# A two-layer diffusion trunk on one core: soft pauses for the modulation's steps, an earlier place for layer 1's, and layer 0's first query projection beside the values

## The chip, the core and the metric

The kernel runs on one core of one Trainium2 chip. The metric is the device time of one execution in microseconds (us), lower is better. Before the change the median of 3 runs is 2235.13 us (2232.56 to 2236.04).

## What is computed

The reference is one inference step of a trunk of two layers, each with its own weights, on 128 prompt tokens and 512 latent tokens (640 columns here), with D = 1024 channels in fp32:

```python
def trunk_layer(x, cond, p, ctx):
    mod = jax.nn.silu(cond) @ p['w_mod'] + p['b_mod']
    sh1, sc1, g1, sh2, sc2, g2 = [m[:, None, :] for m in jnp.split(mod, 6, axis=-1)]
    h = rms_norm(x, p['g_attn']) * (1 + sc1) + sh1
    a, new_ctx = mixer_sublayer(h, p, ctx)
    x = x + g1 * a
    h = rms_norm(x, p['g_ffn']) * (1 + sc2) + sh2
    x = x + g2 * conv_ffn(h, p)
    return x, new_ctx
```

`mod`, the **modulation**, is six vectors of 1024 numbers for each of two conditions; its matrix is 1024 by 6144, 24 MB for each layer. The mixer projects h to the inputs of three branches (a: neighbourhood attention, b: grouped-query attention, c: gated linear attention, which takes `qc`, `kc`, `vc`, `rc`), gates the three results, adds them and projects the sum with `w_out`. `conv_ffn` is an up projection to 2 x 2816 channels, a convolution of width 3, a gate, and a down projection.

## The kernel before

**Layout.** Activations lie with channels on the 128 partitions and the 640 tokens in the free dimension, as 8 blocks. A large product is made of three fp32r matmuls (high x high, high x low, low x high parts), 320 columns wide; weights are loaded as 512 KB tiles by the SP queue, split into a high part on ACT and a low part on DVE or POOL (`Weights.fetch`, `make`, L564), a few tiles ahead of use.

**Who sets the order.** The program is written as streams, Python generators which yield what they wait for: a tile, a free buffer, or an `Event` (L195) with a time. `Order` keeps a modelled clock for each engine, and `Order.one` (L355) picks the next stream: the first in order of priority (0 before 1 before 2 before 3) whose waits are over at the modelled TensorE time, or else the one whose waits end first. The engines then run the instructions in the order so chosen; the model's times are not the chip's. The main stream has priority 2. `Order.later` (L324) gives an event so many ns after the present TensorE time, a **pause**.

**Buffers.** `U` hands out 49 work buffers of 128 x 648 fp32 (4 more at times). A stream that finds none free waits for one to be given back. PSUM has the banks `MM` (2, with 4 more in some stages), `TB` (2) and `S2`.

**The modulation.** `Mod.first` (L748) makes layer 0's first two vectors in four quarters, at the program's start. `Mod.rest` (L782) makes others: `ring` is two pairs of work buffers, each pair holding one block k of one vector (two loads of 256 KB), and a fifth buffer `ms` collects the sums, five `U` buffers held to the end. One step takes two blocks k: it waits for all four loads and for the pause, issues 4 matmuls for each block (128 partitions, 32 columns of weights, 256 columns, one on each quarter of the array), then asks for the next two blocks. After the eighth block `finish` (L825) transposes the vector (two transposes, `modt`) into `modT`. For layer 0, `rest` makes four vectors with a pause of 4000 ns at priority 1. For layer 1 it makes all six, 48 blocks, through `next_mod` (L2285): it begins when `calm` is set, just before the first `bb` product of layer 0's branch b (L1829), with priority 3 and no pause; when the FFN reaches the second of its five parts of the down projection, `rush` (L2154) makes `hurry` (L2292) raise it to priority 1 with a pause of 2000 ns.

```python
            for i in range(0, len(todo), 2):
                v, k0 = todo[i]
                yield ring[0] + ring[1] + [cT, od.later(self.pause)]
```

**The stages.** In each layer: the norm gives h in blocks (`modulate`); `mixer` (L1702) first makes the values and gate inputs, `vz`, block by block of h as the blocks come; then `qc`, `kc`, `rc` twice, and the rest of the branches; branch b ends with `bb`; then the output projection `wo`; then the FFN: two raw blocks (`up`), a norm and `factors` (L931), the other blocks as `pair_x`, `pair_w`, `pair_y` with `pair_act` (L2060), and `dn`, the down projection, whose last part leads into the next layer. In layer 1 the first `qc` and `kc` are made ahead of the norm (`evac_raw`); in layer 0 they come behind `vz`.

Of the kernel before, what the change touches and what calls it, by code (L numbers as in the profile page):

```python
# [18 lines left out]
P = 128  # L19
D = 1024  # L20
KC = 8
# [4 lines left out]
HT = 320  # L26
# [106 lines left out]

def weight_plan(plan, l):

    full = slice(0, D)
    cols = lambda c0, n=P: slice(c0, c0 + n)
    at = lambda nm, r, c: (nm, l, r, c)
    one = lambda c0: plan.plain([at("w_in", full, cols(c0))], KC)
    first = [c0 + p * P for p in range(2) for c0 in (1536, 1792, 2304)]  # L140
    early = NRAW if l else 0
    for c0 in first[:early]:
        one(c0)
    for kk in range(4):
        r = cols(kk * 256, 256)
        plan.plain([at("w_in", r, cols(2048, 256)), at("w_in", r, cols(2560, 32))], 2)
    for c0 in first[early:]:
        one(c0)
    for i in range(KC):
        one(4640 + i * P)  # L150
    for p in range(2):
        for c0 in (0, 256, 512):
            one(c0 + p * P)
    for i in range(0, KC, 4):
        plan.plain([at("w_branch_c", slice(0, 256), cols(i * P, 4 * P))], 2)
    for c0 in (1280, 1408, 768, 896, 1024, 1152):
        one(c0)
    for c0, nm, nk in ((2592, "a", 2), (3616, "b", 4)):
        for kind, i in branch_steps(nm):
            if kind == "g":  # L160
                one(c0 + MERGE[i] * P)
            elif i % (KC // nk) == 0:
                plan.plain([at("w_branch_" + nm, slice(0, nk * P), cols(MERGE[j] * P)) for j in range(i, i + KC // nk)],
                           nk)
    for o in range(KC):
        plan.plain([at("w_out", full, cols(o * P))], KC)
    up = lambda c: [at("ffn_w_up", full, cols(c * P))]
    for step in ffn_steps():
        if step[0] == "raw":
            plan.plain(up(step[1] + step[2] * NFF), KC)  # L170
        elif step[0] == "dn":
            b0, nb = FFN_PARTS[step[1]]
            plan.plain([at("ffn_w_down", cols(b0 * P, nb * P), cols(step[2] * P))], nb)
        else:
            i = step[1]
            plan.pair(step[0], (l, "up", i), (up(i), up(i + NFF)), KC)
# [17 lines left out]

class Event:  # L195
    time = INF


class Slot:
# [65 lines left out]
class Order:  # L265
# [55 lines left out]
        e.time = t  # L321
        return e

    def later(self, ns):  # L324

        return self.moment(self.at["PE"] + ns)

    def start(self, gen, prio):
        self.seq += 1
        self.streams.append([prio, self.seq, gen, ()])  # L330
        self.streams.sort(key=lambda s: s[:2])

    def lift(self, gen, prio):
        for s in self.streams:
            if s[2] is gen:
                s[0] = prio
        self.streams.sort(key=lambda s: s[:2])

    def step(self, s):
# [13 lines left out]
            self.one()  # L353

    def one(self):  # L355
        now, best, at = self.at["PE"], None, INF
        for s in self.streams:
            r = max((self.ready(x) for x in s[3]), default=0.0)
            if r <= now:
                best = s  # L360
                break
            if r < at:
                best, at = s, r
        if best is None:
            raise RuntimeError("streams wait for each other: " + str(
                [(s[2].__name__, [getattr(x[0], "tag", x) if isinstance(x, tuple) else type(x).__name__ for x in s[3]])
# [12 lines left out]
def kernel(ctx: ExitStack, tc: tile.TileContext, I, O, depth=2):  # L379
# [359 lines left out]

    class Mod:  # L740
        def __init__(self, l, pc=None, ready=None):
            self.l, self.pc, self.ready, self.pause = l, pc, ready, 0.0 if l else 4000.0
            self.T = prm.tile([P, 48, 2], F32, tag="modT", bufs=2, name=f"modT{l}")
            self.gsc = prm.tile([P, 2, KC, 2], F32, tag="gsc", bufs=2, name=f"gsc{l}")
            self.have = [Event() for _ in range(24)]
# [2 lines left out]
        def first(self, q):  # L748
# [28 lines left out]
            yield [acc]  # L777
            act(ms[:, :P], acc[:, :P])
            del acc
            yield from self.finish(ms, pieces, P, 256)  # L780

        def rest(self, vectors, after, whole):  # L782

# [11 lines left out]

            fetch(0)
            fetch(1)
            for i in range(0, len(todo), 2):  # L800
                v, k0 = todo[i]
                yield ring[0] + ring[1] + [cT, od.later(self.pause)]
                if k0 == 0 or not whole:
                    acc = yield from TB("mod")
                    psum_names.add(acc.ap.tensor.name)
                a, b = (0, KC - 1) if whole else (k0, k0 + 1)
                for j in range(2):
                    for g in range(4):
                        mm(acc[32 * g:32 * g + 32, :256], cT[:, k0 + j, :], ring[j][g // 2][:, g % 2 * 256:g % 2 * 256 + 256],
                           k0 + j == a, k0 + j == b, tile_position=(0, 32 * g))  # L810
                if not whole or k0 == KC - 2:
                    yield [acc]
                    if whole or k0 == 0:
                        act(ms[:, :256], acc[:, :256])
                    else:
                        tt(ms[:, :256], acc[:, :256], ms[:, :256], ADD)
                    del acc
                for j in range(2):
                    if i + 2 + j < len(todo):
                        yield [od.until(ring[j][1].ap)]  # L820
                        fetch(i + 2 + j)
                if k0 == KC - 2:
                    yield from self.finish(ms, (v * D,), 256, D)

        def finish(self, ms, pieces, n, wide):  # L825
            t = yield from TB("modt")
            yield [ms, self.ready]
            nx = n // P
            for x in range(nx):
# [872 lines left out]
    def mixer(l, h, pc, wg, raws, full, finish, calm):  # L1702
# [12 lines left out]
        merged = tiles8("xm", "mg", NT, F32)  # L1715
        od.start(side.serve(ub, NUX), 0)

        acc = []
        for t in range(5):
            acc.append((yield from MM("vz")))  # L1720
        for kk in range(4):
            w = yield from ws.next()
            for k in range(2):
                kx = kk * 2 + k
                yield [h.done[kx]]
                for t in range(5):
# [2 lines left out]
                    mm(o, h.hi[kx][:, c], w[0][:, k], kx == 0, False)  # L1729
                    mm(o, h.hi[kx][:, c], w[1][:, k], False, False)  # L1730
                    mm(o, h.lo[kx][:, c], w[0][:, k], False, kx == KC - 1)
        vc = [(yield from U("vc0")), (yield from U("vc1"))]
        zT = yield from U("zTs")
        zdone = Event()
# [5 lines left out]
        for p in range(2):  # L1740
# [1 line left out]
                q, k = ready  # L1742
                ready.clear()
            else:
                q = yield from U("qc")
                w = yield from ws.next()
                yield from proj_halves(w, X, KC, evac_to(q, 0.125), "qc")
                k = yield from U("kc")
                w = yield from ws.next()
                yield from proj_halves(w, X, KC, evac_to(k), "kc")  # L1750
# [367 lines left out]
        z = yield from pair_act(i, c, pc, ah)  # L2118
        yield from keep_split(i, z, ah, al, have)

    def ffn(l, x, raws, h, pc, mod, ss, nxt, nraws, rush):
        ah, al = {}, {}
        have = [Event() for _ in range(NFF)]
        pairs = {}
# [11 lines left out]
        for step in ffn_steps():  # L2136
# [13 lines left out]
            elif kind == "dn":  # L2150
                part, o = i, step[2]
                b0, nb = FFN_PARTS[part]
                if part == 1:
                    rush.time = 0.0  # L2154
                ks = range(b0, b0 + nb)
                a = [ah.get(k) for k in ks], [al.get(k) for k in ks]
                while None in a[0]:
# [58 lines left out]
    def program():  # L2216
# [20 lines left out]
        for l in range(depth):  # L2237
# [3 lines left out]
            if l == 0:  # L2241
                yield [h.done[0]]
            if l == 0:
                od.start(mod.rest((2, 3, 4, 5), mod.have[3], False), 1)
            nxt = None
            if l + 1 < depth:
                nxt = Mod(l + 1)
            lazy = next_mod(nxt, calm)
            od.start(lazy, 3)
            od.start(spill(x, h.done[KC - 1]), 1)  # L2250
            full, x = [Event() for _ in range(KC)], [None] * KC

# [21 lines left out]
                ss, nraws = SumSq(), Raw()  # L2274
            else:
                ss = nraws = None
            rush = Event()
            if nxt is not None:
                od.start(hurry(nxt, lazy, rush), 1)
            yield from ffn(l, x, raws, h, pc, mod, ss, nxt, nraws, rush)  # L2280
            raws = nraws
            if nxt is not None:
                mod, pc, wg = nxt, nxt.pc, nxt.wg
# [1 line left out]
    def next_mod(nxt, after):  # L2285
        yield [after]
        if nxt is not None:
            nxt.pc, nxt.wg, nxt.ready, work = load_params(nxt.l)
            od.start(work, 1)
            yield from nxt.rest(range(6), after, True)  # L2290

    def hurry(mod, lazy, when):  # L2292
        yield [when]
        mod.pause = 2000.0
        od.lift(lazy, 1)

    def spill(x, ready):
        yield [ready]
# [65 lines left out]
```

## Time and profile before

| | |
|---|---|
| median of 3 runs | 2235.13 us (2232.56 to 2236.04) |
| the profiled execution's own time | 2225.76 us |
| its span | 2224.0 us |
| TensorE, share of the span busy | 95% |
| VectorE, ScalarE, GpSimd | 70%, 50%, 10% |
| mean granted TensorE clock | 0.989 of full speed |
| DMA | 209.33 MB, mean 94 GB/s |

In the rows PE is TensorE's matmuls, PEld its weight loads, DVE VectorE, ACT ScalarE, POOL GpSimd, SP the engine that issues most DMAs. A row of the timeline has start and duration in us, engine, line, operation, tile written and tiles read, how many instructions are merged, and in brackets the engine's idle time before and who ended it. An fp32 matmul leaves two records, so a block of the modulation leaves 8 (`x8`), and the two transposes of a vector (`modt`) 2.

### The profile page before, as it was taken

To read this page: it belongs to the slowest core of one execution; us is meant where nothing else is said; L and a number is where in the kernel's file an instruction comes from. 1 tells how busy PE (TensorE), PEld (TensorE's weight loads), DVE (VectorE), ACT (ScalarE), POOL (GpSimd) and SP (SyncE) were. 2 spreads that over 40 slices of the span, in tenths; PEclk is the share of its full clock that TensorE was granted. 3 is DMA by queue.
4 is the path that set the end of the run, shared out by engine and by line. 5 is a ranking of instruction groups with operands and counts; after the bars stand their busy time and mean duration, and the time that the engine had idled before them with its cause. 6 is when DMAs were issued, how large, how long until landed. Compare 5 with 4: busy or idle time off the path is not lost. (4 is left out here: it accounts for less than half of the span.)

```text
span 2224.0 us, 40076 instructions
## 1 busy us (share of the span) xinstructions
PE 2113.6 (95%) x16208; PEld 1978.6 (89%) x16208; DVE 1561.9 (70%) x2827; ACT 1122.2 (50%) x2063; POOL 212.6 (10%) x283
## 2 busy tenths in 40 slices
PE   6999999999998968999999999999999989999999
PEld 4878988899997826999998989888999988999999
DVE  5376679673579804978777876787745798687785
ACT  4355755553356402544556667455532575445452
POOL 0201010000120001010010110100001200100101
PEclk9999999999999989999999999999999999999999
DMA  9752221112324373222223112211114212232212
GB/s 307 258 182 76 69 64 50 39 48 69 112 81 152 112 246 107 90 78 94 77 65 133 62 54 70 72 51 39 39 57 133 76 39 68 76 98 71 95 65 91
DMA packets 85874, 209.33 MB, mean 94 GB/s; under 512 B 9590, under 2 KB 22518, under 8 KB 85688
## 3 DMA queue, kind: packets, MB, share of 16 engines
q1 hardware_dynamic: 84472, 204.66, 28.7%
q8 instruction: 128, 2.10, 0.4%
q0 software_dynamic: 1216, 2.10, 0.3%
q14 instruction: 58, 0.48, 0.1%
HBM read 197.81 MB, written 10.98 MB: 94 GB/s over the span
## 5 line engine op out<-in xcount | busy, mean ns | idle before, releaser
L454 ACT ACTIVATE w_h<-w_st 128x1024 fp32r<-128x1024 f32 (+4 forms) x292 | 273.7, 940 | 220.0 <-PE dn L445 57.5
L470 DVE TENSOR_TENSOR w_h<-w_st,w_h 128x1024 fp32r<-128x1024 f32 (+4 forms) x253 | 276.7, 1095 | 140.1 <-ACT w_h L454 133.9
L445 PE MATMUL dn<-a_hi,w_h 128*128 128x320 f32 x1408 | 321.4, 310 | 1.1 <-ACT a_hi L454 1.1
L445 PE MATMUL pair_x<-f,w_h 128*128 128x320 f32 x1440 | 230.1, 311 | 11.1 <-ACT f L454 5.7
L445 PEld LDWEIGHTS dn<-a_hi,w_h 128*128 128x128 f32 x1408 | 239.4, 189 | 1.3 <-ACT a_hi L454 1.3
L445 PEld LDWEIGHTS pair_x<-f,w_h 128*128 128x128 f32 x1440 | 216.1, 189 | 14.1 <-ACT f L454 5.9
L445 PE MATMUL dn<-a_lo,w_h 128*128 128x320 f32 x704 | 218.4, 310 | 2.6 <-DVE a_lo L470 2.6
L445 PEld LDWEIGHTS dn<-a_lo,w_h 128*128 128x128 f32 x704 | 133.2, 189 | 2.8 <-DVE a_lo L470 2.8
L482 DVE SCALAR_TENSOR_TENSOR x<-dn,modT,x 128x128 f32<-128x128 f32 (+2 forms) x240 | 97.2, 434 | 54.4 <-PE dn L445 54.1
L445 PE MATMUL gc<-h_hi,w_h 128*128 128x320 f32 x512 | 131.8, 324 | 2.1 <-ACT mg L454 2.1
L445 PE MATMUL ga<-h_hi,w_h 128*128 128x320 f32 x512 | 125.9, 316 | 0.0
L473 POOL TENSOR_TENSOR w_h<-w_st,w_h 128x1024 fp32r<-128x1024 f32 (+3 forms) x39 | 78.3, 2008 | 470.8 <-ACT w_h L454 308.4
L445 PE MATMUL gb<-h_hi,w_h 128*128 128x320 f32 x512 | 119.0, 312 | 0.0
L445 PE MATMUL wo<-m_hi,w_h 128*128 128x320 f32 x768 | 113.0, 309 | 0.0
L445 PEld LDWEIGHTS wo<-m_hi,w_h 128*128 128x128 f32 x768 | 112.8, 188 | 0.0
L445 PE MATMUL mod<-mod,cT 128*32 128x256 f32 x640 | 76.0, 412 | 31.1 <-DMA mod<-in_w_mod_dram 29.8
L445 PEld LDWEIGHTS gc<-h_hi,w_h 128*128 128x128 f32 x512 | 89.0, 189 | 9.5 <-ACT mg L454 3.1
L445 PEld LDWEIGHTS mod<-mod,cT 128*32 128x32 f32 x640 | 21.1, 111 | 78.2 <-DMA mod<-in_w_mod_dram 65.2
L445 PEld LDWEIGHTS ga<-h_hi,w_h 128*128 128x128 f32 x512 | 88.1, 188 | 2.4 <-issue 2.4
L454 ACT ACT_TABLE_LOAD x64 | 82.1, 1283 | 16.0 <-PE hss L445 11.1
L445 PEld LDWEIGHTS gb<-h_hi,w_h 128*128 128x128 f32 x512 | 86.8, 188 | 1.6 <-issue 1.4
L445 PE MATMUL pair_x<-f_hi,w_h 128*128 128x320 f32 x320 | 79.3, 316 | 5.7 <-ACT up_a L454 5.7
(414 smaller groups left out, 5350.4 us busy)
## 6 DMA issues: line engine op xcount, KB each, us to landing
w_st<-in_wt_dram SPq DMA_DIRECT2D x204, 512.0 KB, 3.4
mod<-in_w_mod_dram SPq DMA_DIRECT2D x160, 256.0 KB, 3.8
w_st<-in_wt_dram SPq DMA_DIRECT2D x48, 320.0 KB, 3.0
mod_w<-in_w_mod_dram SPq DMA_DIRECT2D x32, 256.0 KB, 6.4
xd<-x SPq DMA_DIRECT2D x16, 320.0 KB, 6.0
x<-xd SPq DMA_DIRECT2D x16, 320.0 KB, 3.2
w_st<-in_wt_dram SPq DMA_DIRECT2D x16, 256.0 KB
w_st<-in_wt_dram SPq DMA_DIRECT2D x16, 192.0 KB, 2.5
```

The lines of the kernel that those rows point to most:

```text
L445: nc.tensor.matmul(out, lhsT, rhs, start=start, stop=stop, **kw)
L454: r = nc.scalar.activation(out=out, in_=in_, func=f, **kw)
L470: nc.vector.tensor_tensor(out, a, b, op=op)
L473: nc.gpsimd.tensor_tensor(out, a, b, op=op)
L482: nc.vector.scalar_tensor_tensor(out=out, in0=a, scalar=s, in1=b, op0=op0, op1=op1)
```

## The change

Pauses of the modulation become `Soft` events. `Order.one` looks first for a stream that is ready with all its waits; when there is none, it looks again and leaves soft waits out, so a stream that waits for its pause alone is taken before TensorE would stand idle. Layer 1's modulation gets priority 1 and a pause of 3000 ns from `calm` on, and takes one block k at a time (`n = 1`), while the other half of the ring is being loaded; `rush`, `hurry` and `lift` go. Layer 0's keeps two blocks and 4000 ns, now soft. In layer 0 the first `qc` weight tile moves to the front of the weight plan, ahead of those of `vz`; its 6 matmuls for each block of h are issued behind the 15 of `vz`, into the two `TB` banks, and its separate pass behind `vz` goes. `Mod.first` takes an `MM` bank for its transposes instead of a `TB` bank.

```diff
--- before.py
+++ after.py
@@ weight_plan @@
-    early = NRAW if l else 0
+    early = 2 if l else 1
@@ beside Event @@
+class Soft(Event):
+    pass
@@ Order @@
-    def later(self, ns):
-
-        return self.moment(self.at["PE"] + ns)
+    def later(self, ns, kind=Event):
+
+        e = kind()
+        e.time = self.at["PE"] + ns
+        return e
...
-    def lift(self, gen, prio):
-        for s in self.streams:
-            if s[2] is gen:
-                s[0] = prio
-        self.streams.sort(key=lambda s: s[:2])
...
     def one(self):
-        now, best, at = self.at["PE"], None, INF
-        for s in self.streams:
-            r = max((self.ready(x) for x in s[3]), default=0.0)
-            if r <= now:
-                best = s
-                break
-            if r < at:
-                best, at = s, r
+        now = self.at["PE"]
+        for kinds in ((), Soft):
+            best, at = None, INF
+            for s in self.streams:
+                r = max((self.ready(x) for x in s[3] if not isinstance(x, kinds)), default=0.0)
+                if r <= now:
+                    return self.step(s)
+                if r < at:
+                    best, at = s, r
@@ Mod @@
-            self.l, self.pc, self.ready, self.pause = l, pc, ready, 0.0 if l else 4000.0
+            self.l, self.pc, self.ready = l, pc, ready
...
-            yield from self.finish(ms, pieces, P, 256)
+            yield from self.finish(ms, pieces, P, 256, MM)
...
-        def rest(self, vectors, after, whole):
+        def rest(self, vectors, after, pause, whole):
...
-            for i in range(0, len(todo), 2):
+            n = 1 if whole else 2
+            for i in range(0, len(todo), n):
                 v, k0 = todo[i]
-                yield ring[0] + ring[1] + [cT, od.later(self.pause)]
+                yield [t for j in range(n) for t in ring[(i + j) % 2]] + [cT, od.later(pause, Soft)]
...
-                for j in range(2):
-                    if i + 2 + j < len(todo):
-                        yield [od.until(ring[j][1].ap)]
-                        fetch(i + 2 + j)
-                if k0 == KC - 2:
+                for j in range(i, i + n):
+                    if j + 2 < len(todo):
+                        yield [od.until(ring[j % 2][1].ap)]
+                        fetch(j + 2)
+                if end:
                     yield from self.finish(ms, (v * D,), 256, D)
...
-        def finish(self, ms, pieces, n, wide):
-            t = yield from TB("modt")
+        def finish(self, ms, pieces, n, wide, bank=None):
+            t = yield from (bank or TB)("modt")
@@ mixer @@
+        q0 = None
+        if raws is None:
+            q0 = yield from U("qc")
+            wq = yield from ws.next()
+            ws.held.remove(wq)
+            pq = yield from tbb.several("qc")
+            psum_names.update(p.ap.tensor.name for p in pq)
...
                     mm(o, h.lo[kx][:, c], w[0][:, k], False, kx == KC - 1)
+                if q0 is not None:
+                    for i in range(2):
+                        c = slice(i * HT, (i + 1) * HT)
+                        mm3(pq[i][:, :HT], wq, h.hi[kx][:, c], h.lo[kx][:, c], kx, slice(0, P), kx == 0, kx == KC - 1)
+        if q0 is not None:
+            ev = evac_to(q0, 0.125)
+            for i in range(2):
+                od.start(ev(i, pq.pop(0)), 0)
+            del wq, ev
...
-                q = yield from U("qc")
-                w = yield from ws.next()
-                yield from proj_halves(w, X, KC, evac_to(q, 0.125), "qc")
+                if q0 is None:
+                    q = yield from U("qc")
+                    w = yield from ws.next()
+                    yield from proj_halves(w, X, KC, evac_to(q, 0.125), "qc")
+                else:
+                    q, q0 = q0, None
@@ ffn @@
-                if part == 1:
-                    rush.time = 0.0
@@ program @@
-                od.start(mod.rest((2, 3, 4, 5), mod.have[3], False), 1)
+                od.start(mod.rest((2, 3, 4, 5), mod.have[3], 4000.0, False), 1)
...
-            lazy = next_mod(nxt, calm)
-            od.start(lazy, 3)
+            od.start(next_mod(nxt, calm), 1)
...
-            rush = Event()
-            if nxt is not None:
-                od.start(hurry(nxt, lazy, rush), 1)
-            yield from ffn(l, x, raws, h, pc, mod, ss, nxt, nraws, rush)
+            yield from ffn(l, x, raws, h, pc, mod, ss, nxt, nraws)
@@ next_mod, hurry @@
-            yield from nxt.rest(range(6), after, True)
-
-    def hurry(mod, lazy, when):
-        yield [when]
-        mod.pause = 2000.0
-        od.lift(lazy, 1)
+            yield from nxt.rest(range(6), after, 3000.0, True)
```

## Rows read from the trace of the kernel before

**Rows 1.** The page: the span, and TensorE's busy time, share and matmul count.

```profile
span 2224.0 us, 40076 instructions
PE 2113.6 (95%) x16208; PEld 1978.6 (89%) x16208; DVE 1561.9 (70%) x2827; ACT 1122.2 (50%) x2063; POOL 212.6 (10%) x283
```

**Rows 2.** Busy time by stretch: length, engines' busy us, PE clock, DMA share, GB/s.

```profile
782.00:856.00 74.00, 47.11 (x291) 12.33 (x290) 3.55 (x24) 3.06 (x7) 3.57 (x5) 0.91 0.74 235
```

**Rows 3.** Timeline of PE at both ends of that stretch.

```profile
782.68 1.07 PE L445 MATMUL mod<-mod,cT 128*32 128x256 f32 x16
...
786.76 0.62 PE L445 MATMUL mod<-mod,cT 128*32 128x256 f32 x4 [2.04 <-DMA mod<-in_w_mod_dram]
...
854.35 0.44 PE L450 MATMUL modt<-cn,mod 128*128 128x128 f32 x2 [0.54 <-ACT mod L454]
855.48 0.42 PE L445 MATMUL pair_x<-f_hi,w_h 128*128 128x320 f32 x1 [0.70 <-ACT up_a L454]
```

**Rows 4.** Timeline of POOL there.

```profile
850.74 0.10 POOL L2069 MEMSET up_a<- 128x2 f32 x1 [72.88 <-PE mod L445]
```

**Rows 5.** Busy time by stretch of the modulation's instructions alone: PE, PEld, DVE, ACT.

```profile
677.00:692.00 15.00, 8.58 (x64) 2.15 (x64) 0.00 (x0) 0.38 (x1) 1.00 0.76 239
692.00:782.00 90.00, 3.52 (x50) 1.53 (x50) 0.00 (x0) 0.00 (x0) 0.98 0.38 120
782.00:856.00 74.00, 45.91 (x282) 11.32 (x282) 0.00 (x0) 1.92 (x5) 0.91 0.74 235
```

**Rows 6.** Groups by tile, layer 0, then 1: ns min/median/max, first and last start.

```profile
L445 PE MATMUL bb<-ob_hi,w_h x128: 306/309/313, 540.7 to 589.8; 128*128 128x320 f32 x128
L445 PE MATMUL dn<-a_hi,w_h x704: 302/309/318, 756.2 to 1176.5; 128*128 128x320 f32 x176
...
L445 PE MATMUL bb<-ob_hi,w_h x128: 302/309/313, 1661.6 to 1710.8; 128*128 128x320 f32 x128
L445 PE MATMUL dn<-a_hi,w_h x704: 303/309/468, 1865.5 to 2220.0; 128*128 128x320 f32 x176
```

**Rows 7.** Timeline of PE around a vector's transposes and one step (two blocks).

```profile
695.06 0.38 PE L450 MATMUL modt<-cn,mod 128*128 128x128 f32 x2
695.38 1.07 PE L445 MATMUL mod<-mod,cT 128*32 128x256 f32 x16
696.38 0.41 PE L445 MATMUL pair_x<-f_hi,w_h 128*128 128x320 f32 x1
```

**Rows 8.** Timeline of PE where layer 1's FFN begins.

```profile
1803.92 0.63 PE L445 MATMUL pair_x<-f,w_h 128*128 128x320 f32 x1 [5.65 <-ACT f L454]
1807.79 0.90 PE L445 MATMUL pair_x<-f,w_h 128*128 128x320 f32 x2 [3.24 <-DVE f L470]
```

**Rows 9.** DMA issues, us to landing: 540 to 650 us, then 85 to 160 us.

```profile
w_st<-in_wt_dram SPq DMA_DIRECT2D x17, 512.0 KB, 3.6
...
mod<-in_w_mod_dram SPq DMA_DIRECT2D x39, 256.0 KB, 4.0
w_st<-in_wt_dram SPq DMA_DIRECT2D x7, 512.0 KB, 5.5
```

**Rows 10.** Busy time by stretch; then PE's wait for modulation loads, 45 to 300 us.

```profile
64.00:110.00 46.00, 45.75 (x330) 38.10 (x331) 18.43 (x32) 18.60 (x32) 10.99 (x14) 0.96 0.76 254
...
PE mod L445 <- DMA mod<-in_w_mod_dram: 2.0, 1, 2.0
```

**Rows 11.** The start: one stretch as in rows 2, then PE's timeline.

```profile
26.00:45.00 19.00, 15.97 (x220) 12.63 (x212) 10.00 (x28) 6.03 (x13) 0.00 (x0) 1.00 0.92 310
...
48.76 0.40 PE L445 MATMUL vz<-w_h,h_lo 128*128 128x288 f32 x1 [1.10 <-DVE h_lo L482]
...
56.71 0.41 PE L445 MATMUL qc<-h_hi,w_h 128*128 128x320 f32 x1
...
64.25 2.92 PE L445 MATMUL mod<-mod,cT 128*32 128x256 f32 x16 [1.98 <-DMA mod<-in_w_mod_dram]
...
69.53 0.31 PE L445 MATMUL kc<-h_hi,w_h 128*128 128x320 f32 x1
```

More of the change, by code (lines that the diff above doesn't have):

```diff
@@ L806, in rest @@
                 a, b = (0, KC - 1) if whole else (k0, k0 + 1)
-                for j in range(2):
+                for k in range(k0, k0 + n):
                     for g in range(4):
-                        mm(acc[32 * g:32 * g + 32, :256], cT[:, k0 + j, :], ring[j][g // 2][:, g % 2 * 256:g % 2 * 256 + 256],
-                           k0 + j == a, k0 + j == b, tile_position=(0, 32 * g))
-                if not whole or k0 == KC - 2:
+                        mm(acc[32 * g:32 * g + 32, :256], cT[:, k, :],
+                           ring[(i + k - k0) % 2][g // 2][:, g % 2 * 256:g % 2 * 256 + 256], k == a, k == b,
+                           tile_position=(0, 32 * g))
+                end = k0 + n == KC
+                if end or not whole:
                     yield [acc]
@@ L817, in rest @@
                     del acc
-                for j in range(2):
-                    if i + 2 + j < len(todo):
-                        yield [od.until(ring[j][1].ap)]
-                        fetch(i + 2 + j)
-                if k0 == KC - 2:
+                for j in range(i, i + n):
[3 more added lines that the diff above has]
+                if end:
                     yield from self.finish(ms, (v * D,), 256, D)
-        def finish(self, ms, pieces, n, wide):
-            t = yield from TB("modt")
+        def finish(self, ms, pieces, n, wide, bank=None):
+            t = yield from (bank or TB)("modt")
             yield [ms, self.ready]
@@ L2119, in pair_split, with ffn @@
         yield from keep_split(i, z, ah, al, have)
-    def ffn(l, x, raws, h, pc, mod, ss, nxt, nraws, rush):
+    def ffn(l, x, raws, h, pc, mod, ss, nxt, nraws):
         ah, al = {}, {}
```

## The prediction

> **What bounds the kernel now.** I began with the page: TensorE is busy 95% of the span [rows 1], so there seems to be little to win but the other 5%. That share is an average, and the page's 40 slices show one place near the middle where DVE and ACT thin out. So I asked for busy time by stretch, and one stretch stands alone: in 782 to 856 us TensorE shows 47.11 us of 74 busy, DVE 3.55, ACT 3.06, and the granted clock is 0.91 [rows 2]. The timeline of TensorE says what it does there: from 782.68 to 855.48 us it runs the modulation of layer 1 and nothing else, in pieces, each waiting for its load, the longest for 2.04 us [rows 3]. Why does the FFN not go on beside it? POOL's timeline answers: the memset that opens the next block's `up_a` sat for 72.88 us until a modulation matmul released it [rows 4]. `up_a` took over a buffer that the modulation had held. The work buffers had run out, with five of them in the modulation's hands to its end, and the FFN, which needs two for each block's `up_a` and `up_g`, stood still until the last vectors were through. So the bound of this stretch is a **buffer shortage**, ended by a chain of loads: 72.8 us in which work of a few tens of us is done.
>
> How much is it really? The modulation alone, by stretch, tells where layer 1's 48 blocks lay: 64 records, then 50 (2 of them transposes), then 282 (10 transposes) [rows 5]; at 8 records a block that is 8, 6 and 34 blocks, 48 in all. So 34 blocks ran in 72.8 us, **2.14 us each**.
>
> A second measure needs no reading of causes. From the first `bb` to the last `dn`, the two layers issue the same matmuls. Layer 0 takes 540.7 to 1176.5 us, 635.8; layer 1 takes 1661.6 to 2220.0 us, 558.4 [rows 6]. The **77.4 us** between them are what layer 1's modulation costs now, since layer 1 has none to make.
>
> **The change part by part: layer 1's modulation.** It starts at the same event, the first `bb` at 540.7 us, but now at priority 1, so a block comes whenever 3.0 us of TensorE's planned time have passed. Other streams give way only between groups of six matmuls, under 0.9 us, so the pitch is 3.0 to 3.9 us of other work. From 540.7 to 782.68 us there are 242 us, less the 12 us of modulation in them [rows 3, 5], say 230: room for 59 to 76 blocks where 48 are needed. So it should end, and give its five buffers back, before the place of the shortage. All 96 loads move with it, from a crowded stretch into 540 to about 710 us.
>
> Price of a block. The step at 695.38 us, two blocks among other matmuls, took TensorE 1.00 us until the next product's start [rows 7], 0.50 a block. Taken singly, a block pays for its own changeover; the row bounds it from below at 0.50. From above, the bulk shows 0.62 us for half a block [rows 3], 1.24 a block, at the lower clock and with one load missing. I take **0.60**, near the row with the same neighbours. A vector's transposes cost 0.38 [rows 7], six of them 2.3 us. Sum: 48 x 0.60 + 2.3 = 31.1 us.
>
> By the layers' difference the gain is 77.4 - 31.1 = 46.3 us. By the stall itself: 72.8 us go, and 34 blocks with five vectors' ends come back elsewhere, 34 x 0.60 + 5 x 0.38 = 22.3, a gain of 50.5. The two differ because in layer 1 TensorE idles 5.65 and 3.24 us for the factors at the FFN's begin [rows 8], a gap which layer 0 fills with blocks. What is late there next is that chain of factors on ACT and DVE, and the soft pause lets blocks fall into it. I take the middle, **48 us**. With blocks at 0.50 it is 51 to 54, with all at 1.24 it is 16 to 29.
>
> What it could wake: the loads share the DMA engines with the weights. In 540 to 650 us, 17 weight tiles of 512 KB landed in 3.6 us each; in 85 to 160 us, beside 39 modulation loads, 7 tiles took 5.5 us [rows 9]. There, though, TensorE was busy 45.75 us of 46 at 254 GB/s, and from 45 to 300 us it waited once for a modulation load, 2.0 us [rows 10]. The new stretch would carry less: 17 tiles in 110 us are 81 GB/s, and a block (512 KB) each 4.2 us another 125. A load is asked for two blocks, some 7 us, before its use, and lands in 4.0 [rows 9]. On SP each fetch waits for its block's matmuls, and weight loads stand behind it; they are issued tiles ahead of use. I cost all this at 0; the cover is that lead.
>
> **The first query projection.** Its pass goes: from 56.71 us to `kc` at 69.53 are 12.8 us, of which a modulation step and its wait take 4.9 [rows 11], so 7.9. Its 48 matmuls come back behind `vz`'s, and are hidden where TensorE idles for h: 3.0 us in 26 to 45 us, and 1.1 at 48.76 [rows 11]. So 3.8 us stay bare. The weight tile of 0.5 MB moves ahead in a stretch that runs at 310 GB/s [rows 11], which may put the loads behind it, of `vz` and `mod_w`, and with them h, 1.6 us later. Sum: 7.9 - 3.8 - 1.6 = **2.5 us** won; with nothing hidden 1.6 lost, with all of it hidden and no delay 7.9 won. Its split on ACT and DVE moves too and lies in their idle time there. Its outputs hold both `TB` banks, so layer 0's first modulation step waits for them; nothing needs it soon. The start's transposes in an `MM` bank make the next quarter's matmuls wait for one small DVE read; loads end that stretch, so 0. Layer 0's soft pauses can save the 1.98 us wait [rows 11] or add one like it: 0, with 2.0 either way.
>
> **The sum** is 48 + 2.5 = 50.5 us, against the profiled execution of 2225.8, so 2175. That execution is 9.4 us below the median of the runs; I carry the difference over to the median: 2235.1 - 50.5 = **2184.6 us**.
>
> **The rivals.**
>
> *The shortage comes before the end.* The blocks start late (they need eight free buffers at `calm`), or the pauses stretch, and the FFN again stops with blocks left. For: the five buffers are held through the factors' making, where 28 others are taken. Against: the room of 59 to 76 blocks. With 15 left, each at 2.14 instead of 0.60, it costs 23 us: 2208. Chance 0.11.
>
> *The weights come late.* If the 17 tiles of [rows 9] each land 1.9 us later and prefetching covers none of it, TensorE loses 32 us: 2217. Against it stands the busy stretch of [rows 10]. Chance 0.07. The Trainium skill, page "DMA: Bandwidth & Descriptors", section "Issuing engines are not separate DMA queues", speaks for this one and against the change: whatever queue a DMA is issued from, it runs on the same 16 engines and interleaves with the rest. The trace agrees in the landing, 3.6 against 5.5 us, and by that rule alone the sum would be this 2217.
>
> *Slower: each block waits for its own load.* Spread or not, a block is an instruction in TensorE's order, and when its load is late everything behind it waits. If every block cost the 2.14 us of the bulk, 48 of them with the vectors' ends take 105 us, 28 more than the 77.4 now: 2260 with the first part's gain. It decides from (77.4 + 2.5 - 2.3) / 48 = 1.6 us a block. Against: the 7 us of lead, where the bulk had none. Chance 0.04.
>
> *It does nothing.* The stall only moves: the soft pauses bunch the blocks in another place where buffers are short, and what is won is paid there, 2231 to 2239. Chance 0.02; the stretches where the blocks now fall show no idle buffers' owner but the modulation.
>
> **How the numbers follow.** The forecast, with the stall gone and blocks at 0.50 to 0.75, has the rest, 0.76. A change under 0.2%, 4.5 us, is about what a measurement of this kernel can't tell from none. Faster by more: 0.76 + 0.11 + 0.07 = 0.94; same 0.02; slower 0.04. The range begins at 2235 - 54 - 7.9 - 2, about 2171 (the cheapest blocks, some of them free in the gap of [rows 8], and the whole projection hidden), and goes up to 2213, past the partly left stall; it leaves out the late weights, the slower rival, the nothing, and the upper third of the first, 0.17. The end of 1.24 us a block (2217) lies out with them.
>
> **What would show it.** Right: no stretch of the changed profile with TensorE at the modulation alone; no memset on POOL that waits tens of us for it; its 384 records of layer 1 in groups of 8 between `bb` and the first pairs; from `bb` to the last `dn` of layer 0 some 588 us; TensorE's waits for modulation loads below 5 us in all; `qc` records between `vz` ones and `kc` right behind them, about 2.5 us earlier. Wrong: a block of 72 us of modulation at another place, waits on `w_h` behind late loads around 560 to 700 us, or a layer 0 that still takes over 610 us.

## The result, and the profile after

The changed kernel takes 2180.03 us (median of 4, 2177.05 to 2182.53), the kernel before on the same chip 2234.09 (4, 2232.56 to 2236.04). The ratio is **0.9757, 95% interval [0.974, 0.9774]**: 54 us less where 50.5 were forecast, 2180.0 against 2184.6, inside the range. The profiled executions stand only 45.1 us apart (spans 2224.0 and 2178.9); where the other 9 us are is a question of its own, taken up below. Of all executions one, the first of the query projection alone, took 4618 us where its others took 2225 to 2236, and no number below uses it.

The page after, the lines that answer to [rows 1]:

```profile
span 2178.9 us, 40036 instructions
PE 2096.1 (96%) x16208; PEld 1977.3 (91%) x16208; DVE 1575.3 (72%) x2852; ACT 1113.1 (51%) x2045; POOL 203.9 (9%) x276
```

TensorE's share rises by one point and DVE's by two: the page again hardly shows it. The modulation's instructions by stretch (PE, PEld, DVE, ACT busy, clock, DMA share, GB/s) do, against [rows 5]:

```profile
537.00:701.00 164.00, 24.53 (x296) 6.78 (x296) 0.00 (x0) 1.53 (x4) 1.00 0.61 194
701.00:723.00 22.00, 10.73 (x74) 2.86 (x74) 0.00 (x0) 0.38 (x1) 0.92 0.73 227
723.00:780.00 57.00, 2.86 (x26) 0.90 (x26) 0.00 (x0) 0.37 (x1) 1.00 0.31 105
```

At 8 records a block and 2 for a vector's transposes these are 36, 9 and 3 blocks, 48 in all: the last begins at 730.71 us, some 120 ahead of the old end. The stretch of modulation alone is gone, and on POOL no memset for an `up_a` waits on a modulation matmul any more: of those in 700 to 860 us the longest waits 11.26 us, for DVE. The groups by tile, against [rows 6]:

```profile
L447 PE MATMUL bb<-ob_hi,w_h x128: 303/309/416, 537.7 to 596.9; 128*128 128x320 f32 x128
L447 PE MATMUL dn<-a_hi,w_h x704: 302/309/468, 778.0 to 1131.9; 128*128 128x320 f32 x176
...
L447 PE MATMUL bb<-ob_hi,w_h x128: 305/308/313, 1616.4 to 1665.5; 128*128 128x320 f32 x128
L447 PE MATMUL dn<-a_hi,w_h x704: 302/309/468, 1820.6 to 2174.9; 128*128 128x320 f32 x176
```

So the 45.1 us split at these marks: the first `bb` comes 3.0 us earlier; layer 0 takes 594.2 instead of 635.8, **41.6 us** less; from there to layer 1's `bb` 484.5 instead of 485.1; layer 1 558.5 instead of 558.4; the tail is the same. Layer 0's surplus over layer 1 is 35.7 us where 77.4 were, and 31.1 were forecast.

Where are the 35.7? From `bb` to the first `pair_x` layer 0 takes 537.7 to 701.3 us, 163.6, and layer 1 135.2 (1616.4 to 1751.6, the first row below): 28.4 us for 36 blocks and four vectors' transposes. With 0.38 for each of these [rows 7] that is **0.75 us a block**. From there to the first product with `f_hi` layer 0 takes 21.1 us and layer 1 14.9 (the second row): **6.2 us** for nine blocks that lie in the gap of the factors. All behind costs 1.1.

```profile
1751.65 1.48 PE L447 MATMUL pair_x<-f,w_h 128*128 128x320 f32 x9
...
1766.57 0.47 PE L447 MATMUL pair_x<-f_hi,w_h 128*128 128x320 f32 x1
```

Here is one single block in the timeline of TensorE, in the place of the pair in [rows 7]:

```profile
541.05 0.30 PE L447 MATMUL bb<-ob_hi,w_h 128*128 128x320 f32 x1
541.28 0.64 PE L447 MATMUL mod<-mod,cT 128*32 128x256 f32 x8
541.85 0.41 PE L447 MATMUL bb<-ob_hi,w_h 128*128 128x320 f32 x1
542.10 0.31 PE L447 MATMUL bb<-ob_lo,w_h 128*128 128x320 f32 x1
```

The product's own pitch is 0.15 us a matmul, so from 541.05 to 542.10 two steps of it would be 0.30; with the block they are 1.05: 0.75 again. From the block's start to the product's next are only 0.57 us; the other 0.18 lies at the two changes, 0.08 ahead of the block and 0.10 behind the product's first matmul, which takes 0.41. In [rows 7] a pair took 1.00 from its start to the next product; with 0.18 that is 1.18, 0.59 a block.

And the gap, TensorE's timeline from the first `pair_x` on:

```profile
701.30 1.48 PE L447 MATMUL pair_x<-f,w_h 128*128 128x320 f32 x9
702.72 1.07 PE L447 MATMUL mod<-mod,cT 128*32 128x256 f32 x16
706.44 3.05 PE L447 MATMUL mod<-mod,cT 128*32 128x256 f32 x16 [2.65 <-DMA mod<-in_w_mod_dram]
709.97 0.44 PE L452 MATMUL modt<-cn,mod 128*128 128x128 f32 x2 [0.48 <-ACT mod L456]
710.34 0.63 PE L447 MATMUL mod<-mod,cT 128*32 128x256 f32 x4
711.41 0.63 PE L447 MATMUL mod<-mod,cT 128*32 128x256 f32 x4 [0.45 <-DMA mod<-in_w_mod_dram]
712.79 1.24 PE L447 MATMUL mod<-mod,cT 128*32 128x256 f32 x8 [0.75 <-DMA mod<-in_w_mod_dram]
714.85 1.34 PE L447 MATMUL mod<-mod,cT 128*32 128x256 f32 x8 [0.82 <-DMA mod<-in_w_mod_dram]
717.52 2.68 PE L447 MATMUL mod<-mod,cT 128*32 128x256 f32 x16 [1.33 <-DMA mod<-in_w_mod_dram]
720.12 0.72 PE L447 MATMUL pair_x<-f,w_h 128*128 128x320 f32 x3
```

This is the old stall in small: nine blocks in a row, 17 us, the first two with their data at hand, the others waiting 6.0 us in all for loads. Was TensorE idle for the factors anyhow, or did the blocks keep the products waiting? The row for `pair_x` at 720.12 has no wait in brackets, so its input had been there. Since when, DVE's timeline tells: these are the last `f` that any engine wrote ahead of it, and they were done by 709.76 us, 10 us earlier.

```profile
708.08 1.68 DVE L472 TENSOR_TENSOR f<-hv,f 128x320 fp32r<-128x320 f32 x4
```

That nothing else was missing, the run with hard pauses shows. Last, the start, against [rows 11]: the query's matmuls stand between those of the values, and `kc` follows.

```profile
49.07 0.31 PE L447 MATMUL qc<-h_hi,w_h 128*128 128x320 f32 x1
...
58.39 0.31 PE L447 MATMUL qc<-h_hi,w_h 128*128 128x320 f32 x1
58.98 0.39 PE L447 MATMUL kc<-h_hi,w_h 128*128 128x320 f32 x1 [0.28 <-DVE vc L499]
```

`kc` begins 10.5 us earlier than before (69.53), while `bb` is only 3.0 us earlier.

### The profile page after: what moved, and what is told of

It reads as the page before. It is cut to its first block, busy times and chain, and to the rows that moved or that the text cites. A ratio compares the mean times of both kernels' runs of the same rounds, so it can differ in the third digit from the quotient of the medians.

```text
span 2178.9 us, 40036 instructions
## 1 busy us (share of the span) xinstructions
PE 2096.1 (96%) x16208; PEld 1977.3 (91%) x16208; DVE 1575.3 (72%) x2852; ACT 1113.1 (51%) x2045; POOL 203.9 (9%) x276
## 5 line engine op out<-in xcount | busy, mean ns | idle before, releaser
L475 POOL TENSOR_TENSOR w_h<-w_st,w_h 128x1024 fp32r<-128x1024 f32 (+2 forms) x39 | 79.8, 2047 | 564.3 <-ACT w_h L456 436.0
L447 PE MATMUL wo<-m_hi,w_h 128*128 128x320 f32 x768 | 117.5, 311 | 0.0
L484 DVE SCALAR_TENSOR_TENSOR cv_a<-up_g,pc,cv_a 128x641 f32<-128x641 f32 x80 | 72.8, 910 | 12.8 <-ACT cv_a L456 11.3
L484 DVE SCALAR_TENSOR_TENSOR up_g<-up_a,pc,up_g 128x641 f32<-128x641 f32 x80 | 70.9, 886 | 14.2 <-ACT up_g L456 11.8
L447 PE MATMUL ga<-h_lo,w_h 128*128 128x320 f32 x256 | 79.1, 309 | 0.0
```

The source lines that it names most:

```text
L447: nc.tensor.matmul(out, lhsT, rhs, start=start, stop=stop, **kw)
L475: nc.gpsimd.tensor_tensor(out, a, b, op=op)
L484: nc.vector.scalar_tensor_tensor(out=out, in0=a, scalar=s, in1=b, op0=op0, op1=op1)
```

## Experiments

**The kernel before and the changed kernel once more.**

> The kernel before, unchanged, profiled once more. The profiled execution of before was 2225.8 us while its timed runs lie at 2232.6 to 2236.0, and the profile of the changed kernel lies among its timed runs (2180.9 in 2177.1 to 2182.5). Theory: the stretch of modulation alone is bound by loads, and its length differs between executions by several us (72.8 us in the profiled one, some 80 in the slower ones), the rest of the span being the same. Rival: the executions differ everywhere by 0.4%, and the stretch is again within 1 us of 72.8.

Measured: 2229.87 us (2229.4 to 2235.98) beside 2231.59 (2226.56 to 2241.85, 23 runs), ratio 1.0001 [0.9986, 1.0017]. The program alone spreads by 0.7%. The stretch of modulation alone shows a part of it, busy time in [rows 2]'s columns, this execution:

```profile
782.00:856.00 74.00, 50.83 (x282) 13.13 (x282) 2.37 (x19) 1.54 (x4) 0.15 (x2) 0.73 0.74 235
```

Same instructions, same 235 GB/s, but a granted clock of 0.73 instead of 0.91. Products go on at 859.02 us, having stopped at 783.08, where [rows 3] have 855.48 and 782.68: 3.1 us longer, of the 4.1 by which the spans differ. The theory holds for this stretch; the rest of the span is not the same to the us either (beside it layer 0 is 1.5 us longer, layer 1 1.8 shorter).

> The changed kernel, unchanged, as the reference for the runs beside it. Theory: ratio 0.974 to 0.979 against before, bb to the last dn of layer 0 within 2 us of 594.2, a block of the modulation at 0.74 us; first gc of layer 0 at some 108 us and first bb at some 538 us.

Measured: 2179.96 us (2178.4 to 2181.73), ratio 0.976 [0.9745, 0.9775] to 2234.58. Same result, same marks within 0.7 us.

**The parts alone.** The changed kernel without the query projection:

```diff
-    early = 2 if l else 1
+    early = 2 if l else 0
...
-            yield from self.finish(ms, pieces, P, 256, MM)
+            yield from self.finish(ms, pieces, P, 256)
...
-        if raws is None:
+        if False:
```

> The changed kernel without its first part at the start: layer 0's first query projection behind the values again, the start's transposes in a TB bank again; the modulation as changed. Theory: the modulation carries nearly all of the gain; this is 2 to 4 us slower than the changed kernel (about 2183), the first bb at some 541 us instead of 537.7, and from bb to the last dn of layer 0 within 1 us of 594.2. Rival: the projection's part matters little or costs, and this is at or below 2180.

Measured: 2188.69 us, ratio 0.9805 [0.9784, 0.9825]; layer 0 takes 595.3 us, against 594.2 in the changed kernel; `bb` begins at 545.1. So 43 of the 54 us come with the modulation, and by the medians the projection seems worth 8.7, more than thought; but this kernel's start was late, with the first `gc` at 120.2 us, 2.9 later than in the kernel before. And the projection alone, the kernel before with `q0` and its place in the weight plan, run twice, the second time for its profile:

> The kernel before with only the query projection beside the values and the start's transposes in an MM bank; the modulation as before. Theory: 2 to 4 us faster than before (about 2231), first bb at some 537.7 us, and the stretch of modulation alone stays at 70 us or more. Rival: the projection alone wins nothing because the loads that end the start come later, ratio 1.000 or above.

> The kernel before with the query projection beside the values alone, once more for its profile; nothing is left out. Theory: kc begins 10 us earlier than before (59 against 69.5 us), gc at 108, and the attention branches take back 5 to 7 us of it, so the first bb comes at 537 to 538 us and the whole is 2 to 4 us faster than the kernel before; the stretch of modulation alone is still there, 70 to 77 us long, with a granted clock of 0.7 to 0.92. Rival: the lead is kept when nothing else changes; bb at 531 to 533 and 8 to 10 us faster.

Measured: ratio 0.9987 [0.9973, 1.0001], then 0.9981 [0.9969, 0.9993], that is 2.9 and 4.2 us, the first not clear of noise; `gc` starts at 109.3 and `bb` at 538.5 us, near the theory's 108 and 537 to 538. The rival (lead kept) falls. This execution's stretch of modulation, 783.17 to 859.23 us, is the longest of the three seen, at a clock of 0.72:

```profile
782.00:856.00 74.00, 51.14 (x281) 12.78 (x279) 2.36 (x19) 1.54 (x4) 0.58 (x3) 0.72 0.75 236
```

Layer 0 took 644.5 us in it, 8.7 more than in the profile of before: 2.7 ahead of the stretch, 3.3 in it and 2.8 behind it, where the clock stays at 0.92 to 900 us.

**Is it the buffers?** The kernel before, all orders and pauses kept, with two more work buffers; their room comes from the pool that lends buffers at times, now 1 instead of 3 to the weights and 3 instead of 4 to the work:

```diff
-    NW, NWX, NUX = 9, 3, 4
-    CAP, CAPX = 3, 6
+    NW, NWX, NUX = 9, 1, 3
+    CAP, CAPX = 3, 4
...
-    NU = 49
+    NU = 51
```

> The kernel before with its whole order of streams, its priorities 3 and then 1 and its hard pauses, but with 51 work buffers instead of 49; the room comes from the weights' extra buffers in the FFN, 1 instead of 3 (and 4 loads in flight instead of 6). Theory (shortage): the FFN finds buffers for up_a and up_g, so the stretch of modulation alone goes, without any soft pause; layer 0's bb to dn falls from 635.8 to some 590 to 600 us, the kernel to some 2185 to 2200, less what fewer weight buffers cost, to be read in layer 1's stretch (558.4 before). Rival (the modulation's own late loads and the raise to priority 1 hold TensorE): the order is as before, so a stretch of 50 us or more of modulation alone stays, and the time is 2225 or more.

Measured: 2189.4 us, ratio 0.9809 [0.9786, 0.9833]. Layer 0 takes 595.3 us, to 0.1 us what the early modulation alone gave, with the modulation as low in priority as before and later still: some 29 of its blocks (242 records, with four vectors' transposes) lie in 860 to 1000 us, among products.

```profile
L445 PE MATMUL bb<-ob_hi,w_h x128: 305/308/312, 541.8 to 590.8; 128*128 128x320 f32 x128
L445 PE MATMUL dn<-a_hi,w_h x704: 302/309/417, 755.1 to 1137.1; 128*128 128x320 f32 x176
```

The fewer weight buffers cost 1.6 us in layer 1 (560.0 instead of 558.4). So for the stall it was not the modulation's place that mattered, but the buffers that it held.

**What does the soft pause do?** In the changed kernel every pause hard, so that a block waits for its time even when TensorE would stand idle:

```diff
-        for kinds in ((), Soft):
+        for kinds in ((),):
```

> The changed kernel with all pauses hard again, in both layers (TensorE's planned time must pass also where nothing else is ready); priority, start, 3000 ns and one block at a time as changed. Theory (what matters is that the blocks are done before the buffers run out): ratio within 0.3% of the changed kernel run beside it; layer 0's bb to dn within 4 us. Rival (the softness carries the gain by filling gaps): the blocks leave the gap in front of the factors, fall behind it, and the kernel is 6 us or more slower than the changed one.

Measured: **2166.87 us**, ratio 0.9703 [0.9689, 0.9717], 13 us faster than the change; neither theory nor rival. Layer 0 takes 582.9 us. Its timeline of TensorE in the gap:

```profile
702.57 1.48 PE L447 MATMUL pair_x<-f,w_h 128*128 128x320 f32 x9
703.98 1.07 PE L447 MATMUL mod<-mod,cT 128*32 128x256 f32 x16
707.60 1.31 PE L447 MATMUL mod<-mod,cT 128*32 128x256 f32 x8 [2.55 <-DMA mod<-in_w_mod_dram]
709.38 1.71 PE L447 MATMUL mod<-mod,cT 128*32 128x256 f32 x8 [0.46 <-DMA mod<-in_w_mod_dram]
711.57 0.69 PE L452 MATMUL modt<-cn,mod 128*128 128x128 f32 x2 [0.48 <-ACT mod L456]
711.91 1.15 PE L447 MATMUL pair_x<-f,w_h 128*128 128x320 f32 x3
```

Same entry, four blocks instead of nine, and the products go on at 711.91 instead of 720.12 us, again without a wait, while DVE is still at the same four `f` (710.44 to 712.12 us here). In the changed kernel these `f` were written 2.4 us earlier, so there some 10 us of blocks stood in front of ready products. Of the 11.3 us that layer 0 gives, 7.1 lie in the gap (14.0 instead of 21.1) and 4.2 behind it, where TensorE waits 1.1 us for `a_lo` and `a_hi` instead of 4.3. Layer 0's softness is no part of this: the two traces have every matmul in the same order, layer 0's modulation included, up to the fifth block of this gap.

**The pause's length and the size of a step.** Layer 1's pause 6000 instead of 3000 ns, soft:

> The changed kernel with 6000 ns for 3000 as layer 1's pause. Theory (shortage): at some 6.7 to 7.3 us a block, 22 to 24 blocks are done before the gap at the factors, some 9 in it, the rest meets the shortage; 8 to 12 blocks are made at 2.1 us each with nothing beside them, so a stretch of modulation alone of 15 to 25 us comes back and the kernel is 10 to 18 us slower than the changed one (about 2190 to 2198). Rival (any pause at priority 1 will do): within 4 us of it.

Measured: 2187.55 us, ratio 0.9797 [0.978, 0.9813], 7.6 us slower than the change, less than expected. By records (90, with one vector's transposes) 11 blocks lie in 690 to 715 us, at a clock of 0.80: a longer pause leaves more blocks for the gap. The last four blocks meet the shortage, in a stretch of modulation alone from 803.57 to 812.50 us, where 15 to 25 us had been expected. Two blocks to a step, 6000 ns, soft:

```diff
-            n = 1 if whole else 2
+            n = 2
...
-            yield from nxt.rest(range(6), after, 3000.0, True)
+            yield from nxt.rest(range(6), after, 6000.0, True)
```

> The changed kernel with layer 1's blocks two at a time as before, and 6000 ns of soft pause for each pair. A single block among other matmuls cost 0.74 us by the stretches (bb 59.2 us with 13 blocks against 49.1 with none), where I had 0.60; a pair before cost 1.19 from the last product's start to the second one behind it, 0.59 a block. Theory (the change-over is paid for each interruption): the 36 or so blocks that lie among other matmuls get 0.15 us cheaper, 5 to 6 us faster than the changed kernel (ratio about 0.973 where that one has 0.9757), with waits for modulation loads below 10 us. Rival (one block at a time is there to keep a load in flight): both halves of the ring are asked for at once, the loads land late, TensorE waits some 20 us more and the kernel is 10 us or more slower.

Measured: 2169.16 us, ratio 0.9714 [0.97, 0.9729], 11 us faster than the change, twice what was expected; the gap is 16.5 us here instead of 21.1. Both together, pairs and hard pauses:

> The changed kernel with hard pauses and with layer 1's blocks two at a time after 6000 ns; nothing is left out. Theory: the two gains are independent. A block in a pair costs 0.59 us and a single one 0.74, so 48 blocks give 7 us, and the hard pause spares the run of blocks in the gap of the factors, which was 13 us in singles. Pairs with soft pauses gave 2169.2 and singles with hard ones 2166.9, so some of both is the same gap; I expect 2160 us, within 3, from the first bb product to the last dn of layer 0 576 to 580 us, the gap from the first pair_x to the first product with f_hi 14 to 16 us with two to four blocks in it. Rival: the gain of the pairs came from the gap alone; then this is 2166 to 2169, and the stretch of bb lasts as long as with singles, 59 us.

Measured: **2162.07 us** (2160.82 to 2164.73), ratio **0.968 [0.9666, 0.9695]**, the fastest version seen, 18 us under the change. Layer 0 takes 575.0 us (537.2 to 1112.2). The theory's time holds; its picture of the gap doesn't, as that is 5.1 us long with one step of two blocks in it:

```profile
698.09 1.48 PE L447 MATMUL pair_x<-f,w_h 128*128 128x320 f32 x9
699.50 1.07 PE L447 MATMUL mod<-mod,cT 128*32 128x256 f32 x16
700.50 0.71 PE L447 MATMUL pair_x<-f,w_h 128*128 128x320 f32 x3
701.05 2.30 PE L447 MATMUL pair_y<-f,w_h 128*128 128x320 f32 x12
703.19 0.31 PE L447 MATMUL pair_x<-f_hi,w_h 128*128 128x320 f32 x1
```

From `bb` to the first `pair_x` are 160.9 us, 25.4 over this kernel's layer 1, with 40 blocks and five vectors: (25.4 - 1.9) / 40 = **0.59 us a block** in pairs. The waits from 537 to 760 us have none for a load of the modulation:

```profile
PE pair_x L447 <- DVE w_h L472: 2.0, 1, 2.0
PE pair_x L447 <- DVE f_lo L472: 1.9, 1, 1.9
PE pair_x L447 <- ACT f_hi L456: 0.7, 1, 0.7
```

The 2.6 us for `f_lo` and `f_hi` lie right behind the gap, so a part of the waiting has only moved there; the 2.0 for a weight come at 723 us. The factors are also further on in this kernel: the last `f` ahead of the three matmuls at 700.50 were done 2.2 us behind the first `pair_x` (DVE, 700.33), where the changed kernel has 8.5. Why they come earlier with pairs is open, so not all that the pairs gain is shown to be the price of a block.

**What is the projection worth beside hard pauses?** The first diff of the parts on top of the hard pauses:

> The changed kernel with hard pauses and without the query projection beside the values; nothing of the computation is left out. Beside the kernel with hard pauses (2166.9) it gives the projection's worth a second time. Theory: the 8 to 10 us seen between the changed kernel and the one without the projection were partly an unlucky start of that kernel (its first gc was 3 us later than that of the kernel before, with the same instructions up to there); the projection is worth 3 to 5 us, so 2170 to 2172, with the first bb at 541 to 543 us. Rival: the projection is worth 8 to 10 us beside the early modulation, so 2175 to 2177 and bb at 545.

Measured: 2173.19 us, ratio 0.9729 [0.9714, 0.9743], 6.3 us over the kernel with hard pauses: between theory and rival. Layer 0 takes 582.9 us in both, `bb` starts at 542.9 against 538.9. So four values, 2.9, 4.2, 6.3 and 8.7 us, and at the mark `bb` 1 to 4 us, but 7 to 8 in the pair whose one start was late. Some 3 to 6 us is what they allow when that pair is left out; nearer it isn't settled.

**When the buffers run out after all.** Single blocks, hard pauses of 6000 ns:

> The changed kernel with single blocks, hard pauses and 6000 ns for layer 1; nothing is left out. It makes the rival in which buffers run out before the blocks do: at a block each 6.7 us some 12 to 14 of the 48 are left when the FFN wants its buffers. Theory: these come as a run with TensorE at the modulation alone, each at about 2.1 us instead of 0.74, so 17 to 20 us are added to the 2166.9 of the kernel with 3000 ns, 2184 to 2192, with a stretch of 25 to 30 us without other products after 770 us and a POOL memset that waits for it. Rival: the pause is now the wait, as nothing else may run, and each of them takes up to 6 us: 2215 to 2235. If no such run shows, 2165 to 2170, and the lack of buffers didn't come from the modulation's.

Measured: 2193.33 us, ratio 0.9821 [0.9805, 0.9836], a little over the theory's 2184 to 2192, and far from its rival. The stall is back, from 791.77 to 822.98 us with 14 blocks (112 records), 2.2 us each. Its two ends on TensorE, then the memset on POOL:

```profile
791.77 1.07 PE L447 MATMUL mod<-mod,cT 128*32 128x256 f32 x16
795.28 1.07 PE L447 MATMUL mod<-mod,cT 128*32 128x256 f32 x4 [2.44 <-DMA mod<-in_w_mod_dram]
...
822.41 0.58 PE L452 MATMUL modt<-cn,mod 128*128 128x128 f32 x2 [0.55 <-ACT mod L456]
823.54 0.64 PE L447 MATMUL pair_x<-f_hi,w_h 128*128 128x320 f32 x1 [0.56 <-ACT up_a L456]
```

```profile
818.77 0.10 POOL L2093 MEMSET up_a<- 128x2 f32 x1 [33.22 <-PE mod L447]
```

It costs 26.5 us over the hard pauses of 3000 ns. The soft pause with the same 6000 ns, 2187.55, is 6 us better: in these two pairs of kernels softness pays where the pause is too long for the room, and costs where it fits.

## Why the prediction was right, and where not

**The bound**: right. A shortage of buffers it was, shown from both sides: two more buffers alone win what moving the modulation wins, and 14 blocks left over bring the stall back.

**Room for the blocks**: right. The blocks came one in 4.5 us (163.6 / 36), 3.8 of them other work, inside the 3.0 to 3.9 of the forecast, and 45 of 48 were through by 723 us. The first rival (the shortage comes before the end) did not occur, but its price was sound: 23 us for 15 blocks left, 26.5 measured for 14.

**Price of a block**: mis-sized. 0.60 was taken from a step of two blocks, as "near the row with the same neighbours"; a single block pays the change between the two kinds of matmul alone, 0.75, the upper end of what I had allowed for the forecast. Over the 36 blocks ahead of the gap that is 5.4 us. In pairs it is 0.59.

**The gap of the factors**: wrong. "The soft pause lets blocks fall into it" was booked as a credit, and so the middle, 48, was put over the layers' 46.3. The nine blocks there cost 6.2 us, 0.69 each, nearly as much as blocks beside products, since they wait for their loads in front of ready ones. The trace of before had held the sign: there, too, layer 0's gap was filled, with eight blocks, and took 17.8 us (675.95 to 693.75) where layer 1's took 14.9. Layer 0 gave 41.6 us in place of 48, and the 6.4 between are 5.4 for the price, 1.7 for the credit, less 0.7 on the other 12 blocks with two vectors' ends (7.3 where 12 x 0.60 + 2 x 0.38 = 8.0 were charged). The Trainium skill says, on the page "TensorE: Matmul & The Clock Gate", section "Step-by-step: what each phase is for", that only weight loads are pulled ahead and matmuls keep their program order. The trace agrees: `pair_x` stood ready and ran at 720.12 us, behind the last block. I had used the same argument for the slower rival ("everything behind it waits") and not for the gap.

**The loads**: right at 0 outside the gap. In 537 to 665 us, 16 weight tiles land in 4.0 us instead of the 3.6 of [rows 9], beside 56 loads of the modulation, at 209 GB/s:

```profile
mod<-in_w_mod_dram SPq DMA_DIRECT2D x56, 256.0 KB, 3.3
w_st<-in_wt_dram SPq DMA_DIRECT2D x16, 512.0 KB, 4.0
```

The 0.4 us are a fifth of the 1.9 us feared, and TensorE waits for no weight there; the rival falls, and so does the slower one, since between `bb` and the last `dn` no block outside the gap waits. That loads share the same 16 DMA engines and interleave is what the Trainium skill states on the page "DMA: Bandwidth & Descriptors", section "Issuing engines are not separate DMA queues"; the trace agrees, by these 0.4 us. TensorE's waits for modulation loads sum to 6.4 us where "below 5" was forecast, all but 0.4 of them in the gap:

```profile
PE mod L447 <- DMA mod<-in_w_mod_dram: 6.4, 6, 2.7
```

**The projection**: 2.5 forecast, 3.0 at the first `bb`, and 3 to 6 by time. The sum came near for a reason that it didn't hold. At `kc` the lead is 10.5 us and not 2.5: the modulation's step with its wait, 4.9 us, leaves that stretch too, and the pass's matmuls with all delay cost 2.3 us (`kc` at 58.98, the old pass at 56.71) where 3.8 and 1.6 were charged. From `kc` to `bb` the changed kernel then takes 478.7 us instead of 471.2: 2.9 more at the moved modulation steps, some 2.6 in slower matmuls (granted clock 0.93 in 266 to 315 us), about 2 in waits such as `naT` for DVE. That the branches follow their chains on DVE and ACT, and an early start therefore doesn't all come through, fits these numbers but was not tested.

**The carry from profile to median**: a guess that was wrong to make. It was carried over as if the change had nothing to do with it. But the stretch that went is also where executions differ: 72.8 and 75.9 us in two profiles of before and 76.1 in that of the projection alone, at clocks of 0.91, 0.73 and 0.72, and layer 0, slowed beside it too, took 635.8, 640.5 and 644.5. The profiled one was at the cheap end. The other runs of before point the same way: of the 51 on record beside the experiments the two shortest, 2226.0 and 2226.6 us, had a mean granted clock of 0.988, the three longest, 2236.6 to 2241.9, one of 0.978 to 0.980. Where in the span it fell they don't show, so the same cause is likely, not shown. So the change won 45 us against that one and 54 against the median, and two errors, 5.4 us too much against the profile and 9 too little against the median, nearly made up for each other: that the total came so close is luck.

## What to carry to other kernels

Idle time of TensorE is free only until what it waits for is ready: filler whose own load may be late does not give way, and in an engine that keeps program order it delays the work for which the gap was waiting. So put filler where its data are sure to lie ready, in steps large enough to pay the change of instruction kind once, and let it keep its pause. When a stretch shows one engine at work alone, ask who holds the buffers: two more of them, or giving them back earlier, can be worth the same.

## What was not expected

One change from fp32r products to the modulation's fp32 matmuls and back costs about 0.3 us: two single blocks take 1.50, a pair 1.18. A stretch in which TensorE waits for loads between short pieces is dear twice: with the same instructions and the same 235 GB/s its granted clock was 0.91 in one execution, 0.73 and 0.72 in others (means of time at 1.2 and at 2.4 GHz), and in the last of these the products right behind it ran on slowly at first, the first `pair_x` in 0.63 us where [rows 3] show 0.42. The Trainium skill, page "TensorE: Matmul & The Clock Gate", section "HAM oscillation — how this bites in real kernels", says that waits for loads between matmuls let the clock fall back. The traces agree, with the numbers above, and add that the same stretch loses more in one execution than in another.
